# Attention: five of twenty key tiles' probabilities summed on VectorE instead of three, and two more steps ahead of the second maxima's transposes

## The chip, the cores and the metric

The kernel runs on one core of one Trainium2 chip. The metric is the device time of one execution in microseconds. Engines are called PE (TensorE), DVE (VectorE), ACT (ScalarE), POOL (GpSimd) and SP (SyncE, which only issues DMAs here). SBUF is the on-chip memory, PSUM the accumulator memory that PE writes.

## The reference

One layer of a diffusion backbone: a combined projection, attention beside a state space, an output projection and an FFN. 2048 latent and 256 context tokens; attention has 8 query heads, 2 key/value heads and head size 64. All in float32. The change concerns the attention alone, in which a latent query sees 2048 latent keys and 512 cached context keys (20 tiles of 128 keys), a context query the 256 context keys (2 tiles):

```python
def one_block(q_blk):
    s = jnp.einsum("bqkgd,bskd->bkgqs", q_blk, k, preferred_element_type=jnp.float32) * scale
    p = jax.nn.softmax(s, axis=-1).astype(v.dtype)
    return jnp.einsum("bkgqs,bskd->bqkgd", p, v)
```

## The kernel before

The program runs in stages: projections (to about 460 us), attention with the state space's scans beside it (to about 1505 us), the state space's GLU, the output projection, and a long FFN. This section is about the attention stage.

**Units.** Attention is cut into 20 units (`units`, L176): a unit is a pair of heads and a block of 512 latent or 256 context queries. 16 are latent (20 key tiles each), 4 are context units (2 tiles). They are numbered ui = 0 to 19; the context units are 0, 2, 4 and 6, and the last is 19.

**What a unit does.** For each key tile j, `scores` (L260) multiplies keys by queries into PSUM tile st (L267, L268; two matmuls per head, since the operands are split into a rounded part and its remainder), and ACT writes the exponentials into an SBUF tile p of 128 keys x 2 heads x 512 queries (L270). There are 11 buffers of p. `values` (L275) multiplies p with the values into pv (L284; the keys are contracted by PE). The softmax's denominator needs the sum over all p tiles of a unit. It is made by adding the tiles element by element: one running sum on DVE (L294, one 128x1024 add per tile) and one on POOL (L297, two 128x512 adds per tile). The first tile that goes to an engine isn't added; its buffer becomes the running sum. `VJ` (L305) lists the tiles of a latent unit that go to DVE; the last unit has a rule of its own. `finish` (L308) adds the two sums (L313, DVE) and contracts them with ones (L318, PE), takes the reciprocal through a DMA round trip, and scales pv (L336).

**What must be there before a unit starts.** The exponentials need each query's maximum over all keys. `prep` (L179) makes it for the unit ahead: it splits the queries (L219, L222), multiplies them with the keys a second time (L197, PE) and reduces each 128x512 block to a column of maxima (L198, DVE); `pmx` has three PSUM buffers for these blocks. `close` (L201) reduces a head's columns (L204, DVE) and writes the negated maximum into zb (L205, ACT); `put` (L207) transposes zb on PE (L210), and ACT copies it into the lower rows of ql (L211), where it joins the scores' second matmul.

**The order.** In this stage PE and DVE run in the order in which the program is written (`manual_schedule`, L1148); ACT, POOL and SP are ordered by a scheduler. `attend` (L347) writes it: groups of four tiles; first the scores of the next group, then the values of this one, so that the adds of tiles 8 to 11 are written after the scores of tiles 12 to 15. `prep` is a generator, and a `yield` in it is a step; after each score tile (a slot) `attend` lets it go st["per"] steps further, so that the steps of the units ahead are spread over this unit's 20 slots. `prep_steps` (L341) gives their number. The state space (`ssm_gen`, L944) and the GLU's first loads (`glu_front`, L1088) are generators too, one step per slot and one after each group's values.

Of the kernel before, what the change touches and what calls it, by code (L numbers as in the profile page):

```python
# [48 lines left out]
def build(nc, tc, I, O):  # L49
# [129 lines left out]
    def prep(ui, late=0):  # L179
        kv, tok, nq, k0, k1, pr_ = units[ui]  # L180
        khl, kho = KK[kv, k0]
        ntq = nq // 128
        nkc = (k1 - k0 + 3) // 4
        qs = X["kc"].tile([128, 4, 2, 2, 64], F32, name="qs", bufs=1)
        for h in range(2):
            src = q_scr[tok:tok + nq, 4 * kv + 2 * pr_ + h].rearrange("(i p) d -> p i d", p=128)
            for d in range(2):
                X["dma"].dma_start(out=qs[:, 0:ntq, h, d, :], in_=src)
        res, mxs = [], []

        def maxes(h, cs):
            qh, khl = res[h][0], KK[kv, k0][0]
            for i in range(ntq):
                for c in cs:
                    a, b = 512 * c, min(512 * c + 512, (k1 - k0) * 128)
                    sp_ = X["pmx"].tile([128, 512], F32, name="m")
                    PE.matmul(sp_[:, 0:b - a], qh[:, i * 128:(i + 1) * 128], khl[:, a:b], start=True, stop=True)  # L197
                    V.tensor_reduce(mxs[h][:, i, c:c + 1], sp_[:, 0:b - a], axis=AX.X, op=ALU.max)  # L198
                    yield

        def close(h):  # L201
            z = X["zb"][h % 2]
            m4 = X["kc"].tile([128, 4], F32, name="m4", bufs=2)
            V.tensor_reduce(m4[:, 0:ntq], mxs[h][:, 0:ntq, 0:nkc], axis=AX.X, op=ALU.max)  # L204
            S.activation(z[:, 0:ntq, 64], m4[:, 0:ntq], AF.Copy, scale=-1.0)  # L205

        def put(h):  # L207
            tp = X["pmx"].tile([128, 512], F32, name="m")
            for i in range(ntq):
                PE.transpose(tp[:, i * 128:(i + 1) * 128], X["zb"][h % 2][:, i, :], ident)  # L210
            S.copy(res[h][1][64:128, 0:nq], tp[64:128, 0:nq])  # L211

        yield
        for h in range(2):
            qh, ql = (X["kc"].tile([128, nq], F32R, name=f"{n}{h}_{nq}", bufs=2 if nq > 256 else 1) for n in ("qh", "ql"))
            tp = X["pmx"].tile([128, 512], F32, name="m")
            for i in range(ntq):
                PE.transpose(tp[:, i * 128:(i + 1) * 128], qs[:, i, h].rearrange("p a b -> p (a b)"), ident)
            S.copy(qh[:, 0:nq], tp[:, 0:nq])  # L219
            if ui > 1:  # L220
                yield
            V.tensor_sub(ql[0:64, 0:nq], tp[0:64, 0:nq], qh[0:64, 0:nq].bitcast(F32))  # L222
            res.append((qh, ql))
            mxs.append(X["kc"].tile([128, 4, 6], F32, name="mx", bufs=2))
            yield
        if ui > 1:
            yield from maxes(0, range(nkc))
            close(0)
            second = maxes(1, range(nkc))
            for _ in range(min(6, 2 * nkc)):  # L230
                next(second)
                yield
            put(0)
            yield
            yield from second
            close(1)
            yield
            yield
            yield
            put(1)  # L240
            yield
            QT[ui] = res
            return
        for h in range(2):
            yield from maxes(h, range(nkc - late))
            if not late:
                close(h)
        if late:
            yield "rest"
            for h in range(2):  # L250
                yield from maxes(h, range(nkc - late, nkc))
                close(h)
        for h in range(2):
            put(h)
            yield
        QT[ui] = res
# [18 lines left out]
    def values(ui, j):  # L275
# [14 lines left out]
        else:  # L290
            e = "v" if j in VJ else "g"
        if e in acc:
# [9 lines left out]
            S.copy(pvs[:, 0:nq], pv[:, 0:nq])  # L302
            PEND.append((ui, pvs, acc))

    VJ = (4, 11, 19)  # L305
    PEND = []

    def finish():  # L308
# [31 lines left out]

    def prep_steps(ui):  # L341
        kv, tok, nq, k0, k1, pr_ = units[ui]
        n = 2 * (nq // 128) * ((k1 - k0 + 3) // 4) + 10
        first = next(i for i, u_ in enumerate(units) if (u_[0], u_[3]) == (kv, k0))
        return n + (1 + (k1 - k0 + 3) // 4 if ui == first else 0)

    def attend(B, Sg):  # L347
# [10 lines left out]
        def slot(ui, j):  # L358
            while st["ready"] < ui:
                step()  # L360
            lat = units[ui][2] > 256
            if lat and not j:
                st["goal"] = min(ui + (2 if ui + 1 < 2 * len(cu) else 1), len(units) - 1)
                st["per"] = sum(prep_steps(i) for i in range(st["ready"] + 1, st["goal"] + 1)) / 19.5
                st["q"] = 0.0
            scores(ui, j)
            st["q"] += st["per"] if lat else 0.0
            while st["q"] >= 1.0:
                st["q"] -= 1.0
                if st["ready"] < st["goal"]:  # L370
                    step()
            if lat:
                X["pos"] = "p"
                next(Sg, None)
# [22 lines left out]
    with ExitStack() as pa:  # L397
# [489 lines left out]

        def bg():
            g = dict(c=kbuild(0, 20, 22), k=kbuild(0, 0, 20, (0, 4, 8, 12)), p=prep(0))
            X["dma"] = nc.scalar  # L890
            for ch in "cpk":
# [4 lines left out]
            for ch in "cpkp":  # L896
                next(g[ch])
                yield
            p = prep(1, 1)
            next(p)  # L900
            for ch in "ppkppkk":
# [14 lines left out]
            for ui in range(2, len(units)):  # L916
                kv, k0, k1 = units[ui][0], units[ui][3], units[ui][4]
                if (kv, k0) not in KK:
                    yield from kbuild(kv, k0, k1)
                yield from prep(ui)  # L920
                yield ui
# [797 lines left out]
```

## Time and profile before

| what | value |
|---|---|
| median of 3 runs | 3349.92 us (3345.46 to 3354.12) |
| profiled execution, its own time | 3348.23 us |
| its span, first to last instruction | 3346.3 us |
| mean granted TensorE clock | 0.965 |
| PE busy | 3066.9 us, 92% of the span |
| DVE busy | 2530.4 us, 76% |
| POOL busy | 1933.8 us, 58% |
| ACT busy | 1343.0 us, 40% |

The shares are means over stages with different limits. A row of the profile names an engine, a line of the kernel, the tiles written and read (out<-in) and their sizes; "idle before" is the time for which the engine stood still ahead of the instruction, with what ended it. A granted clock of 1.00 is 2.4 GHz, 0.50 is 1.2 GHz.

### The profile page before, as it was taken

What the parts mean: (1) busy time and instruction counts of PE and PEld (TensorE: products, weight loads), DVE (VectorE), ACT (ScalarE), POOL (GpSimd) and SP (SyncE); (2) the same over time, 40 slices, a digit from 0 to 9 for tenths busy, and PEclk for the clock granted to TensorE, in tenths of its full rate; (3) what the DMA queues carried; (4) which work ended last, traced back from release to release, by engine and by line L of the source; (5) the groups of instructions that cost most, each with busy time, mean ns of one, the idle gap of its engine ahead of it and who ended that gap; (6) DMA issues with size and microseconds to landing.
All of it is one profiled execution on the core that took longest, in us unless ns stands there. A gap on an engine that the chain in (4) does not pass through costs nothing. (4 is left out here: it accounts for less than half of the span.)

```text
span 3346.3 us, 46314 instructions
## 1 busy us (share of the span) xinstructions
PE 3066.9 (92%) x16087; PEld 2479.5 (74%) x16087; DVE 2530.4 (76%) x3414; ACT 1343.0 (40%) x2378; POOL 1933.8 (58%) x1433
## 2 busy tenths in 40 slices
PE   7898888999999999886997999999999999999897
PEld 5787664565655665545776999999999998878686
DVE  4889766767777777667777877887788877567887
ACT  4333333444444444534555433433343434232332
POOL 3777535666785787664434544554455556354675
PEclk9999999999999999998998999999999999999899
DMA  7565442323333322204565444444434445658653
GB/s 264 188 198 186 144 121 49 87 76 86 84 81 87 84 72 50 64 20 145 176 188 190 140 117 120 132 132 121 119 101 125 127 129 169 164 147 201 175 205 138
DMA packets 515380, 435.20 MB, mean 130 GB/s; under 512 B 106374, under 2 KB 449454, under 8 KB 515148
## 3 DMA queue, kind: packets, MB, share of 16 engines
q1 hardware_dynamic: 498060, 400.57, 39.8%
q0 software_dynamic: 5184, 18.88, 3.3%
q10 hardware_dynamic: 11904, 12.82, 1.1%
q8 instruction: 127, 2.08, 0.3%
q14 instruction: 105, 0.86, 0.1%
HBM read 279.37 MB, written 143.73 MB: 126 GB/s over the span
## 5 line engine op out<-in xcount | busy, mean ns | idle before, releaser
L297 POOL TENSOR_TENSOR p<-p 128x512 f32<-128x512 f32 x502 | 699.0, 1431 | 281.5 <-PE pv L284 177.1
L89 POOL TENSOR_TENSOR op<-wr,op 128x512 fp32r<-128x512 f32 (+1 forms) x297 | 413.3, 1398 | 427.9 <-ACT op L88 386.6
L94 PE MATMUL o<-h,op 128*128 128x384 f32 x1848 | 624.0, 338 | 17.1 <-ACT h L88 16.4
L95 PE MATMUL o<-h,op 128*128 128x384 f32 x1848 | 624.2, 338 | 16.4 <-DVE h L89 16.4
L96 PE MATMUL o<-h,op 128*128 128x384 f32 x1848 | 622.8, 337 | 0.0
L198 DVE TENSOR_REDUCE mx<-m 128x1 f32<-128x512 f32 (+1 forms) x656 | 405.2, 674 | 145.4 <-PE m L197 143.7
L270 ACT ACTIVATE p<-st 128x1024 f32<-128x1024 f32 (+1 forms) x328 | 330.3, 1015 | 285.6 <-PE st L268 278.4
L88 ACT CAST op<-sw 128x512 fp32r<-128x512 f32 (+1 forms) x381 | 232.9, 613 | 331.8 <-PE o L95 267.8
L95 PEld LDWEIGHTS o<-h,op 128*128 128x128 f32 x1848 | 351.4, 190 | 18.8 <-DVE h L89 18.6
L94 PEld LDWEIGHTS o<-h,op 128*128 128x128 f32 x1848 | 351.0, 190 | 18.8 <-ACT h L88 17.9
L96 PEld LDWEIGHTS o<-h,op 128*128 128x128 f32 x1848 | 351.2, 190 | 0.0
L89 POOL TENSOR_TENSOR op<-sw,op 128x512 fp32r<-128x512 f32 (+1 forms) x177 | 259.4, 1469 | 121.8 <-ACT op L88 121.8
L88 ACT CAST op<-wr 128x512 fp32r<-128x512 f32 (+1 forms) x333 | 199.0, 608 | 255.9 <-PE o L95 170.4
L284 PE MATMUL pv<-p,vall 128*64 128x512 f32 (+1 forms) x1312 | 296.4, 594 | 0.0
L95 PE MATMUL o<-fvm,op 128*128 128x512 f32 x693 | 278.6, 402 | 18.6 <-DVE fvm L89 9.4
L94 PE MATMUL o<-fvm,op 128*128 128x512 f32 x693 | 277.1, 401 | 10.0 <-ACT fvm L88 8.0
L197 PE MATMUL m<-khl,qh 128*128 128x512 f32 (+1 forms) x656 | 232.8, 425 | 56.4 <-DVE mx L198 47.4
L267 PE MATMUL st<-qh,khl 128*128 128x512 f32 (+1 forms) x656 | 276.4, 422 | 6.7 <-ACT p L270 6.0
L96 PE MATMUL o<-fvm,op 128*128 128x512 f32 x693 | 275.1, 398 | 0.0
L268 PE MATMUL st<-ql,kho 128*128 128x512 f32 (+1 forms) x656 | 259.2, 396 | 0.0
L197 PEld LDWEIGHTS m<-khl,qh 128*128 128x128 f32 x656 | 125.4, 191 | 131.0 <-DVE mx L198 99.8
L284 PEld LDWEIGHTS pv<-p,vall 128*64 128x64 f32 x1312 | 86.9, 137 | 156.8 <-issue 153.6
(314 smaller groups left out, 6287.2 us busy)
## 6 DMA issues: line engine op xcount, KB each, us to landing
wr<-w_ffn_in SPq DMA_DIRECT2D x132, 512.0 KB
wm<-w_mod SPq DMA_DIRECT2D x48, 512.0 KB
act_scr<-s SPq DMA_DIRECT2D x99, 192.0 KB
wr<-act_scr SPq DMA_DIRECT2D x36, 512.0 KB
x_scr<-gy POOLq DMA_DIRECT2D x36, 512.0 KB, 6.4
xt<-x SPq DMA_DIRECT2D x34, 512.0 KB
act_scr<-gy SPq DMA_DIRECT2D x90, 192.0 KB
sw<-act_scr SPq DMA_DIRECT2D x54, 256.0 KB
```

Of the source, the lines that this page charges most:

```text
L88: a = (copy or S.copy)(hi, src)
L89: b = (sub or V).tensor_sub(lo, src, hi.bitcast(F32))
L94: PE.matmul(out, ah, bh, start=first, stop=False)
L95: PE.matmul(out, ah, bl, start=False, stop=False)
L96: return PE.matmul(out, al, bh, start=False, stop=last)
L197: PE.matmul(sp_[:, 0:b - a], qh[:, i * 128:(i + 1) * 128], khl[:, a:b], start=True, stop=True)
L198: V.tensor_reduce(mxs[h][:, i, c:c + 1], sp_[:, 0:b - a], axis=AX.X, op=ALU.max)
L267: PE.matmul(st[:, h, 0:nq], khl[:, kc], qh[:, 0:nq], start=True, stop=False)
L268: PE.matmul(st[:, h, 0:nq], kho[:, kc], ql[:, 0:nq], start=False, stop=True)
L270: S.activation(p[:, :, 0:nq], st[:, :, 0:nq], AF.Exp, scale=0.125)
L284: PE.matmul(pv[64 * h:64 * h + 64, 0:nq], X["vall"][:, k0 + j, 64 * kv:64 * kv + 64], p[:, h, 0:nq], start=j == 0, stop=j == nk - 1)
L297: G.tensor_add(acc[e][:, h, 0:nq], acc[e][:, h, 0:nq], p[:, h, 0:nq])
```

## The change

Two edits. `VJ` gets five tiles instead of three: 3, 7, 11, 15 and 19, the last of each group of four. So the DVE sum starts with tile 3 and has four adds in a unit instead of two; POOL has 14 tiles to add instead of 16, 28 instructions instead of 32. This holds for 15 latent units; the last latent unit and the context units keep their rules. And in `prep` five steps instead of three lie between the second head's `close` and its `put`, with `prep_steps` raised by two.

```diff
@@ prep
             yield from second
             close(1)
-            yield
-            yield
-            yield
+            for _ in range(5):
+                yield
             put(1)
@@ attention
-    VJ = (4, 11, 19)
+    VJ = (3, 7, 11, 15, 19)
@@ prep_steps
-        n = 2 * (nq // 128) * ((k1 - k0 + 3) // 4) + 10
+        n = 2 * (nq // 128) * ((k1 - k0 + 3) // 4) + 12
```

The new file is one line shorter, so that lines behind `prep` have a number lower by one there: L270 is L269, L294 is L293, L313 is L312, L330 is L329, L336 is L335.

DVE in unit 18, from the final sum of unit 17 on, before (mx<-m are the block maxima, m<-mx a head's `close`, p<-p an add of tiles):

```order
L313 TENSOR_TENSOR p<-p 128x1024
L198 TENSOR_REDUCE mx<-m 128x1 x5
L204 TENSOR_REDUCE m_12814<-mx 128x4
L198 TENSOR_REDUCE mx<-m 128x1 x15
L294 TENSOR_TENSOR p<-p 128x1024
L330 RECIPROCAL rr<-rr 128x8
L198 TENSOR_REDUCE mx<-m 128x1 x5
L204 TENSOR_REDUCE m_12986<-mx 128x4
L336 TENSOR_TENSOR pvs<-pvs,rT 128x512
```

The same place now:

```order
L312 TENSOR_TENSOR p<-p 128x1024
L198 TENSOR_REDUCE mx<-m 128x1 x4
L204 TENSOR_REDUCE m_12777<-mx 128x4
L198 TENSOR_REDUCE mx<-m 128x1 x6
L293 TENSOR_TENSOR p<-p 128x1024
L198 TENSOR_REDUCE mx<-m 128x1 x10
L293 TENSOR_TENSOR p<-p 128x1024
L329 RECIPROCAL rr<-rr 128x8
L198 TENSOR_REDUCE mx<-m 128x1 x4
L204 TENSOR_REDUCE m_12950<-mx 128x4
L293 TENSOR_TENSOR p<-p 128x1024
L335 TENSOR_TENSOR pvs<-pvs,rT 128x512
```

Between the final sum and the add of tile 11 stood 20 maxima; now an add (of tile 7) parts them into 10 and 10, and another (of tile 15) stands behind the second `close`.

ACT at the end of unit 9, where the maxima of unit 10 are closed, before (p<-st are the exponentials, zb the negated maxima, ql the copy after `put`):

```order
L270 ACTIVATE p<-st 128x1024 x3
L1007 COPY s<-h_5217 128x4
L1008 ACTIVATE s<-h_5217 128x4
L270 ACTIVATE p<-st 128x1024 x4
L205 ACTIVATE zb_4606<-m_8435 128x4
L211 CAST ql_512_8008<-m 64x512
L270 ACTIVATE p<-st 128x1024
```

The same place now:

```order
L269 ACTIVATE p<-st 128x1024 x3
L1006 COPY s<-h_5217 128x4
L1007 ACTIVATE s<-h_5217 128x4
L269 ACTIVATE p<-st 128x1024 x3
L205 ACTIVATE zb_4606<-m_8417 128x4
L269 ACTIVATE p<-st 128x1024
L211 CAST ql_512_7998<-m 64x512
L269 ACTIVATE p<-st 128x1024
```

zb stood behind the fourth exponential, the unit's last; now it stands ahead of it.

## Rows read from the trace of the kernel before

**Rows 1.** Stretch, us, busy us of PE, PEld, DVE, ACT, POOL; clock, DMA share, GB/s

```profile
460.00:1505.00 1045.00, 958.04 (x4450) 578.85 (x4451) 729.42 (x926) 462.54 (x721) 721.08 (x519) 0.98 0.28 74
```

**Rows 2.** Waits of PE, 460 to 1505 us: total us, times, longest us

```profile
PE m L197 <- DVE mx L198: 43.8, 21, 13.1
PE m L210 <- ACT zb L205: 18.8, 15, 2.7
PE st L267 <- ACT p L270: 6.0, 9, 1.4
```

**Rows 3.** Groups by line, 460 to 1505 us: busy us, mean ns, idle before

```profile
L297 POOL TENSOR_TENSOR p<-p 128x512 f32<-128x512 f32 x502 | 699.0, 1431 | 281.5 <-PE pv L284 177.1 <-ACT p L270 104.5
...
L294 DVE TENSOR_TENSOR p<-p 128x1024 f32<-128x1024 f32 x37 | 82.8, 2239 | 14.4 <-PE pv L284 12.0 <-ACT p L270 2.2
```

**Rows 4.** Timeline of PE: start us, us, instruction, idle before it

```profile
526.09 2.59 PE L197 MATMUL m<-khl,qh 128*128 128x512 f32 x4 [9.66 <-DVE mx L198]
...
1360.88 0.80 PE L197 MATMUL m<-khl,qh 128*128 128x512 f32 x1 [8.59 <-DVE mx L198]
...
1439.76 1.39 PE L197 MATMUL m<-khl,qh 128*128 128x512 f32 x2 [13.09 <-DVE mx L198]
```

**Rows 5.** Timeline of DVE

```profile
511.51 11.65 DVE L294 TENSOR_TENSOR p<-p 128x1024 f32<-128x1024 f32 x1
...
578.75 5.76 DVE L1033 TENSOR_TENSOR s<-s,et 128x584 f32<-128x584 f32 x1
...
1353.97 6.25 DVE L89 TENSOR_TENSOR wgl<-raw,wgh 128x512 fp32r<-128x512 f32 x1 [8.31 <-ACT wgh L88]
...
1400.00 2.30 DVE L313 TENSOR_TENSOR p<-p 128x1024 f32<-128x1024 f32 x1
...
1421.50 17.54 DVE L294 TENSOR_TENSOR p<-p 128x1024 f32<-128x1024 f32 x1
```

**Rows 6.** Timeline of POOL (instructions without a pause between them in one row)

```profile
484.97 37.11 POOL L297 TENSOR_TENSOR p<-p 128x512 f32<-128x512 f32 x30 [11.95 <-PE pv L284]
...
561.02 22.86 POOL L297 TENSOR_TENSOR p<-p 128x512 f32<-128x512 f32 x18 [23.29 <-PE pv L284]
...
1331.04 28.64 POOL L297 TENSOR_TENSOR p<-p 128x512 f32<-128x512 f32 x22 [15.50 <-ACT p L270]
...
1399.94 38.01 POOL L297 TENSOR_TENSOR p<-p 128x512 f32<-128x512 f32 x30 [16.77 <-ACT p L270]
```

**Rows 7.** Timeline of POOL and DVE around 1297 us

```profile
1269.28 46.25 POOL L297 TENSOR_TENSOR p<-p 128x512 f32<-128x512 f32 x32 [6.24 <-PE pv L284]
...
1281.29 1.85 DVE L1053 TENSOR_TENSOR r<-r,rw 128x584 f32<-128x584 f32 x1
...
1297.49 1.46 DVE L294 TENSOR_TENSOR p<-p 128x1024 f32<-128x1024 f32 x1
```

**Rows 8.** Timeline of DVE: maxima behind an idle time, where new adds come to stand

```profile
1226.78 1.36 DVE L198 TENSOR_REDUCE mx<-m 128x1 f32<-128x512 f32 x2 [1.14 <-PE m L197]
...
1285.98 1.36 DVE L198 TENSOR_REDUCE mx<-m 128x1 f32<-128x512 f32 x2 [2.84 <-PE m L197]
...
1414.67 1.36 DVE L198 TENSOR_REDUCE mx<-m 128x1 f32<-128x512 f32 x2 [4.62 <-PE m L197]
```

**Rows 9.** Busy time by stretch, columns as in the first group

```profile
526.10:532.00 5.90, 5.90 (x13) 4.10 (x14) 4.67 (x8) 1.02 (x1) 0.33 (x1) 0.50 0.13 22
...
1439.80:1443.40 3.60, 3.60 (x8) 2.71 (x9) 2.47 (x5) 0.42 (x1) 0.00 (x0) 0.50 0.24 63
```

**Rows 10.** Timeline at the end of unit 9

```profile
867.13 1.95 ACT L270 ACTIVATE p<-st 128x1024 f32<-128x1024 f32 x2 [0.54 <-PE st L268]
...
867.55 0.39 PE L268 MATMUL st<-ql,kho 128*128 128x512 f32 x1
868.98 0.20 ACT L205 ACTIVATE zb<-m 128x4 f32<-128x4 f32 x1
...
869.23 0.66 PE L210 MATMUL m<-ident,zb 128*128 128x128 f32 x4 [1.29 <-ACT zb L205]
```

## Prediction, made before the change was run

> **What bounds the kernel now.** I read the stage first, then the waits inside it, then the rows behind the longest waits. The change touches only the attention stage, from 460 to 1505 us. In that stage TensorE (PE) is busy 958.0 of 1045 us, GpSimd (POOL) 721.1, VectorE (DVE) 729.4 and ScalarE 462.5 [rows 1]. So PE sets the time, and what an edit can win is at most the 87 us in which PE stands still, plus what a lower clock costs behind such gaps. PE's waits say who makes them [rows 2]: 43.8 us for DVE's row maxima (L198), 18.8 us for the zb copy of ScalarE (L205), 6.0 us for the exponentials (L270). None of them names POOL. POOL's 502 half-tile adds at 1431 ns [rows 3] are off PE's path, and taking work from POOL is worth something only through DVE.
>
> That path exists. Three rows hold 31.3 of the 43.8 us: PE waits 9.66, 8.59 and 13.09 us for one maximum each [rows 4]. Each time DVE was inside one single instruction that should take about a microsecond: 11.65 us and 17.54 us for a 128x1024 add (L294), 6.25 us for a 128x512 subtraction (L89); a fourth, L1033 at 578.75, took 5.76 us, and no PE gap follows it [rows 5]. In each case DVE comes free about when a long unbroken row of POOL adds ends: 484.97 + 37.11 = 522.08 against 523.16, 561.02 + 22.86 = 583.88 against 584.51, 1331.04 + 28.64 = 1359.68 against 1360.22, 1399.94 + 38.01 = 1437.95 against 1439.04 [rows 5, 6]. So a DVE instruction with two SBUF operands can be passed over by POOL until POOL has nothing left to do. Mostly it is not: the add at 1297.49 took 1.46 us in the middle of POOL's 46.25 us row [rows 7]. What differs is how long POOL had run undisturbed. At 1297.49 the last two-operand instruction of DVE had ended at 1283.14, 14.4 us earlier, and DVE got its turn. Passed over were those that came 26.5 us after POOL's start (511.51), 17.7 us after it (578.75) and, at 1421.50, 19.2 us after the L313 that ended at 1402.30 [rows 5, 6, 7]. I looked at every such meeting in the stage: none up to 14.4 us is passed over, and beyond 17 us there are only these four. I take that as the rule of this kernel; why the chip does so no row shows.
>
> The Trainium skill states it otherwise (page "SBUF — State Buffer", section "Who interferes with whom"): a DVE instruction with two SBUF inputs contends with a GpSimd instruction that reads SBUF, and the shared ports are an exclusive lock held for one whole instruction, so that the loser waits for that one. By that rule DVE would wait for one POOL add at most, and no number of DVE adds would cure a long wait; the 17.54 us, in which some 13 POOL adds went by, do not agree with it [rows 5]. What the time would be if regular DVE adds cured nothing is the first rival.
>
> **The change part by part.**
>
> *Adds moved from POOL to DVE.* 15 units change (all latent ones but the last). Each loses two tiles on POOL, four half adds: 60 x 1.43 us = 86 us of POOL's time [rows 3], which by itself is worth nothing, since nobody on PE's path waits for it except through the 11 p buffers, which ScalarE's exponentials need free. PE waits 6.0 us for the exponentials [rows 2]. I take half as won, 3 us; the ends are 0 and 6.0.
>
> Each unit gets two more adds on DVE, after tiles 7 and 15 (tile 3 only starts the sum in place of tile 4): 30 adds of 1.2 us free or 2.3 us when a POOL add is in front. Their cover is the burst of 16 value matmuls and the scores behind it, in which DVE waits for PE: after L1053 at 1281.29 it idles 2.84 us [rows 7, 8], which holds 2.3. The tightest place I found is 1226.78, where instructions of the state space leave 1.14 us [rows 8]; there an add costs 2.3 - 1.1 = 1.2 us. At the other new place, the end of a unit, DVE idles longer, since it waits for ScalarE's copy of the next queries. Some three units of 15 are tight: 3 us lost. If the cover were gone everywhere it would be 30 x 1.2 = 36 us, the upper end; the lower is 0.
>
> *What they do to the long waits.* The adds now come after every group of four tiles (7, 11, 15, 19), and the final sum L313 after the next unit's first group, so that DVE meets POOL about every 12 us: below 14.4. I expect the long waits behind PE's three gaps to go.
> - Unit 18, 1421.50: the add of tile 7 lands near 1411, where DVE idled 4.62 us anyway [rows 8]; the add of tile 11 then gets its turn in about 2 us. PE's 13.09 us go whole. So does the half clock behind them: at 1439.80 to 1443.40 PE was busy throughout at a granted clock of 0.50 (1.2 instead of 2.4 GHz), having stood idle before; 3.6 us of work done in 3.6 that take 1.8 [rows 9]. Together 15 us.
> - Unit 1, 511.51: with an add of tile 7 near 497 the add at 511.51 takes 2.3 instead of 11.65 us. Behind it stand L330 and three state-space instructions, which ran beside an idle POOL and would now take some 1.85 us each, as at 1281.29 beside POOL [rows 7]: the maxima resume at 511.5 + 2.3 + 0.2 + 5.55 = 519.6. PE's maximum then comes at about 520 and not at 526.09. 6 us, and of the 2.95 us that the half clock cost (5.90 us at 0.50 [rows 9]) I take 1: 7 us.
> - Unit 17, 1353.97: L89 waited 8.31 us for ScalarE first [rows 5], and still will. Then 2.3 instead of 6.25 us: 4 us, and 1 for the clock: 5 us.
>
> That is 27 us; the ends are 0 (the first rival) and 31.3 + 2.95 + 1.8 = 36 us (the gaps and both half clocks gone).
>
> *Two more steps.* Fifteen times PE waits for zb, 18.8 us in all [rows 2], mostly 1.29 us as at 869.23. There the order tells why: zb stands on ScalarE behind the last two exponentials, 867.13 to 869.08, and PE's transposes come right after the scores of the last of them [rows 10]. The two extra steps, spread over the same 20 slots (52 / 19.5 = 2.67 steps a slot instead of 50 / 19.5 = 2.56), put the last maximum two steps earlier, and on ScalarE zb now goes ahead of the unit's last exponential; I count eight units in which that happens, and some had it already. zb then ends about 0.2 us after the last but one exponential, near 868.3, and PE, done with its scores at 867.94, waits 0.4 instead of 1.29: 0.9 us x 8 = 7, with 1 more for the unit whose wait was 2.7: 8 us. Ends: 0 and 18.8. Nothing is queued behind: the later copy of the put (L211) has a burst of value matmuls before the next scores need it.
>
> **The sum.** -3 + 3 - 27 - 8 = -35 us against the profiled execution's own 3348.2 us: 3313 us. The median of the runs shown is 1.7 us above that execution, less than the rest is uncertain. What follows the stage is tied to its end (the last unit's normalisation frees the memory that the output projection's weights need), so I let the gain through whole.
>
> **The rivals.**
> 1. *The long waits are not cured*, only moved: which of the two engines gets the ports is a matter of phase, or POOL's rows of adds are not the cause. For it: only four cases, and a page that knows no such passing over. Against: no exception among all meetings in the stage. The time: 3348 - 8 - 3 + 3 = 3340.
> 2. *Slower: more adds, more passing over.* If each L294 runs the same risk whatever came before, 2 of 37 were passed over [rows 3, 5], so 30 more bring 1.6 further, each at the cost of the two seen, (9.66 + 13.09) / 2 = 11.4 us and some 2.4 of half clock: 13.8 us. 1.6 x 13.8 = +22, with rival 1's -8: 3362. It decides from the first new add of tile 7 or 15 that lasts over 5 us while PE needs a maximum. Against: the new adds come 12 us after the one before.
> 3. *DVE's queue is the bound*: the adds cost 1.2 us each since the cover is used up. +33 more than taken: 3346. For it: DVE is busy 70% of the stage and PE waits already behind such pile-ups; against: the idle times of [rows 8].
> 4. *The extra steps move nothing on PE's path* (PE waits for the last exponential instead of zb): then 8 us less won, 3321; within the forecast's own range.
>
> **How the numbers follow.** The forecast with its spread (3290 to 3328) gets 0.71, rival 1 0.15, rival 2 0.07, rival 3 0.07. Rival 2 and half of rival 3 may lie outside the range, and some of the far side; 3288 to 3343 leaves out under 2 in 10. A measurement of this kernel can tell about 0.3%, 10 us, from no change, so faster means under 3338: the forecast's 0.71 and half of rival 1 make 0.78. The other half and rival 3 make 0.15 for the same, rival 2 0.07 for slower.
>
> **What would show it.** In the profile after: L297 down to 442 adds and L294 up by 30; no DVE add over about 3 us in units 1, 17 and 18; PE's wait for L198 down from 43.8 to about 20 us, that for zb from 18.8 to about 10. If long DVE instructions remain in the middle of POOL's rows with less than 14.4 us since DVE's last, the rule is wrong and rival 1 or 2 holds. If there are none and PE's wait for L198 has not fallen, rival 3 holds. If the stage shrinks by 35 us and the whole does not, what follows was tied to something else.

## The result and the profile after

The change took 3313.37 us (median of 4 runs, 3312.63 to 3319.35) where the kernel before took 3351.26 beside it (4 runs, 3345.46 to 3354.12): a ratio of 0.9898, 95% interval 0.987 to 0.9926. It is faster, by about 35 us (38 by the medians, 34 by the ratio). The profiled execution's span is 3310.9 us (before 3346.3), its mean granted clock 0.972 (before 0.965).

The first view is the attention stage in one row (us; busy time of PE, PEld, DVE, ACT, POOL; clock; DMA share; GB/s). It answers to [rows 1]: the stage ends near 1480 instead of 1505 us. POOL's busy time fell from 721 to 672 us while DVE's rose from 729 to 751, and PE's stayed at about 960.

```profile
460.00:1480.00 1020.00, 964.00 (x4479) 582.44 (x4480) 750.64 (x961) 464.29 (x725) 671.63 (x459) 0.99 0.29 76
```

The second is PE's waits in that stretch (us in total, times, longest), to be read against [rows 2]: the wait for the maxima fell from 43.8 to 16.5 us and its longest from 13.1 to 3.2, that for zb from 18.8 to 7.2. The wait for the exponentials rose from 6.0 to 8.8.

```profile
PE m L197 <- DVE mx L198: 16.5, 29, 3.2
PE st L266 <- ACT p L269: 8.8, 11, 3.2
PE m L210 <- ACT zb L205: 7.2, 11, 1.3
PE m L1012 <- DVE mx L198: 6.8, 14, 2.3
```

The third is the groups by line (busy us, mean ns), against [rows 3]: 442 adds on POOL instead of 502, and 67 on DVE instead of 37, whose mean fell from 2239 to 1706 ns although there are more of them.

```profile
L296 POOL TENSOR_TENSOR p<-p 128x512 f32<-128x512 f32 x442 | 647.0, 1502 | 286.7 <-PE pv L283 185.7 <-ACT p L269 101.0
...
L293 DVE TENSOR_TENSOR p<-p 128x1024 f32<-128x1024 f32 x67 | 114.3, 1706 | 7.6 <-PE pv L283 5.2 <-ACT p L269 2.2
```

The fourth is DVE's timeline (start, duration, both us) at the places of the long instructions of [rows 5], in units 1, 3, 17 and 18. In this execution none lasts over 3 us: 1.21 instead of 11.65, 2.71 where L1033 took 5.76 at 578.75, 1.47 instead of 6.25, and 1.24 (the add of tile 11 at 1408.04) instead of 17.54. The new adds of tile 7 in units 1 and 18 are those at 498.38 and 1396.56.

```profile
498.38 1.22 DVE L293 TENSOR_TENSOR p<-p 128x1024 f32<-128x1024 f32 x1
...
514.45 1.21 DVE L293 TENSOR_TENSOR p<-p 128x1024 f32<-128x1024 f32 x1
...
568.82 2.71 DVE L293 TENSOR_TENSOR p<-p 128x1024 f32<-128x1024 f32 x1
...
1346.15 1.47 DVE L89 TENSOR_TENSOR wgl<-raw,wgh 128x512 fp32r<-128x512 f32 x1 [6.37 <-ACT wgh L88]
...
1396.56 1.79 DVE L293 TENSOR_TENSOR p<-p 128x1024 f32<-128x1024 f32 x1
...
1408.04 1.24 DVE L293 TENSOR_TENSOR p<-p 128x1024 f32<-128x1024 f32 x1
...
1414.42 2.06 DVE L293 TENSOR_TENSOR p<-p 128x1024 f32<-128x1024 f32 x1
```

POOL's rows beside two of them show that the cure has two halves. In unit 1 the new add at 498.38 breaks POOL's row, and with fewer adds the row ends at 486.08 + 28.25 = 514.33, just ahead of the add at 514.45, which so meets nobody. In unit 3 the add at 568.82 still waits for the row's end, 550.02 + 20.43 = 570.45, as the prediction's rule has it after 18 us without a turn; only the end is near.

```profile
486.08 28.25 POOL L296 TENSOR_TENSOR p<-p 128x512 f32<-128x512 f32 x22 [12.78 <-PE pv L283]
...
550.02 20.43 POOL L296 TENSOR_TENSOR p<-p 128x512 f32<-128x512 f32 x16 [19.01 <-PE pv L283]
```

**Where the time came from.** The table splits each profiled execution. The stage runs from the first score matmul to the last scaling of pv. "Idle" is the sum of PE's gaps in it; "half clock" is half of PE's busy time in the stretches granted 0.50, the time that they cost; "mx" is the part of the idle time that stood ahead of L197, whoever ended it. "Rest" is what follows the stage, up to the end of the span.

| run | stage | idle | mx | zb | half clock | rest |
|---|---|---|---|---|---|---|
| before | 1049.8 | 87.6 | 52.7 | 18.8 | 11.8 | 1838.9 |
| the change | 1020.6 | 56.4 | 26.8 | 7.3 | 11.5 | 1832.4 |
| e1_adds | 1019.9 | 63.0 | 29.5 | 17.0 | 6.8 | 1838.3 |
| e2_steps | 1067.7 | 97.9 | 70.9 | 7.3 | 20.1 | 1843.1 |
| e3_unspaced | 1075.4 | 97.8 | 66.6 | 8.7 | 30.0 | 1836.3 |
| e4_touch | 1046.8 | 79.6 | 49.5 | 7.8 | 16.3 | 1837.9 |
| e5_touch_often | 1067.2 | 92.0 | 57.8 | 18.8 | 20.2 | 1836.3 |
| e7_nine | 1029.0 | 56.1 | 34.7 | 3.1 | 11.6 | 1837.7 |
| e8_change_again | 1016.0 | 54.5 | 25.8 | 7.4 | 8.0 | 1838.8 |
| e10_whole | 1076.9 | 101.1 | 58.4 | 15.9 | 28.4 | 1842.3 |
| e11_change_whole | 1081.3 | 98.0 | 60.8 | 6.2 | 32.9 | 1837.3 |
| e12_touch_wide | 1036.7 | 71.3 | 37.5 | 8.0 | 12.4 | 1840.7 |

A row is one execution, and the experiments ran on four chips, on which the kernel before isn't equally fast. So a difference between rows isn't the edit's alone: e10's span is 30 us longer than that of the kernel before, but its ratio, taken on one chip, says 8 us. e1's row is the fastest of its five runs (3318.43 us, median 3325.99), e2's lies 11 us above its median.

The stage gave 29.2 us and the rest 6.4. Matching PE's instructions one by one, the change is 11 us ahead behind unit 1's gap, loses 5 again between 600 and 750 us, wins 6 at unit 17 and 16 at unit 18.

The 5 us that are lost show what a new add costs where little covers it. DVE's timeline of the change: the new add of a tile 7 took 2.31 us beside POOL at 711.26, and from there on DVE had no idle time up to the add of tile 11 at 723.12, behind which a scaling and a state-space product queue.

```profile
711.26 2.31 DVE L293 TENSOR_TENSOR p<-p 128x1024 f32<-128x1024 f32 x1
...
723.12 2.29 DVE L293 TENSOR_TENSOR p<-p 128x1024 f32<-128x1024 f32 x1
...
727.12 1.73 DVE L1052 TENSOR_TENSOR r<-r,rw 128x584 f32<-128x584 f32 x1
```

The same three queue in the kernel before, at 730.88 and as long, but there DVE had idled 1.65 and 0.47 us ahead of them, and PE's wait behind them was 0.51 us. Its DVE timeline:

```profile
724.07 1.36 DVE L198 TENSOR_REDUCE mx<-m 128x1 f32<-128x512 f32 x2 [1.65 <-PE m L197]
...
730.88 2.33 DVE L294 TENSOR_TENSOR p<-p 128x1024 f32<-128x1024 f32 x1
```

PE's timeline in the change: it stood still for 2.27 us, waiting for a maximum.

```profile
729.50 1.56 PE L1012 MATMUL m<-ut,mst 128*128 128x144 f32 x8 [2.27 <-DVE mx L198]
```

Behind this gap, and behind one of 3.21 us at 1058, PE worked at 0.50 (1.2 GHz). The stretches (columns as in the first view):

```profile
730.30:733.70 3.40, 3.40 (x12) 2.91 (x11) 0.81 (x2) 1.82 (x4) 3.40 (x4) 0.50 0.19 41
1061.40:1064.80 3.40, 3.40 (x8) 2.72 (x9) 2.27 (x4) 2.81 (x4) 0.00 (x0) 0.50 0.89 204
```

So the long half-clock stretches behind units 1, 17 and 18 are gone ([rows 9] are two of them), but new short ones took their place: the stage lost 11.5 us to them instead of 11.8.

### The profile page after: what moved, and what is told of

The parts are those of the page before. It is cut to its first block, busy times and chain, and to the rows that moved or that the text cites. A ratio compares the mean times of both kernels' runs of the same rounds, so it can differ in the third digit from the quotient of the medians.

```text
span 3310.9 us, 46264 instructions
## 1 busy us (share of the span) xinstructions
PE 3059.0 (92%) x16087; PEld 2468.7 (75%) x16087; DVE 2547.8 (77%) x3444; ACT 1341.8 (41%) x2378; POOL 1888.8 (57%) x1373
## 5 line engine op out<-in xcount | busy, mean ns | idle before, releaser
L296 POOL TENSOR_TENSOR p<-p 128x512 f32<-128x512 f32 x442 | 647.0, 1502 | 286.7 <-PE pv L283 185.7
L269 ACT ACTIVATE p<-st 128x1024 f32<-128x1024 f32 (+1 forms) x328 | 331.4, 1016 | 245.5 <-PE st L267 236.3
L197 PE MATMUL m<-khl,qh 128*128 128x512 f32 (+1 forms) x656 | 230.0, 422 | 30.5 <-DVE mx L198 20.2
L197 PEld LDWEIGHTS m<-khl,qh 128*128 128x128 f32 x656 | 124.3, 191 | 103.5 <-DVE mx L198 67.7
```

The source lines that it names most:

```text
L269: S.activation(p[:, :, 0:nq], st[:, :, 0:nq], AF.Exp, scale=0.125)
L296: G.tensor_add(acc[e][:, h, 0:nq], acc[e][:, h, 0:nq], p[:, h, 0:nq])
```

## The experiments

Theory: what counts is how long POOL runs without a two-operand DVE instruction between; the change is faster since its adds come at every fourth tile. Rivals: it is the smaller load on POOL, or the two steps. Line numbers in experiments with five steps are those of the change, as far as the first line that an experiment adds. Each ratio is to the kernel before on the same chip, where its medians were 3356 us (e1 to e4), 3359 (e5, e7, e8), 3371 (e10, e11) and 3358 (e12).

**e1_adds: the five tiles alone, three steps as before.**

```diff
-    VJ = (4, 11, 19)
+    VJ = (3, 7, 11, 15, 19)
```

> The five tiles on DVE alone, three steps as before. Theory (spacing: a two-operand DVE instruction is passed over only after some 15 us of undisturbed POOL adds): the long waits in units 1, 17 and 18 go, PE's wait for L198 falls from 43.8 to about 20 us, PE's wait for zb stays near 18.8 us; 3320 to 3328 us, about 25 us under the kernel before. Rival (the two steps made most of the gain): less than 12 us under it, 3338 or more.

3325.99 us, ratio 0.991 (0.989 to 0.9931). PE's waits (same columns as above):

```profile
PE m L197 <- DVE mx L198: 17.7, 20, 3.5
PE m L210 <- ACT zb L205: 17.0, 15, 1.3
```

The maxima's wait falls as in the change, zb's stays. The tiles alone bring most of the gain (0.991 against the change's 0.9898, and 0.9879 in its second measurement, e8).

**e2_steps: the two steps alone.**

```diff
-            yield
-            yield
-            yield
+            for _ in range(5):
+                yield
...
-        n = 2 * (nq // 128) * ((k1 - k0 + 3) // 4) + 10
+        n = 2 * (nq // 128) * ((k1 - k0 + 3) // 4) + 12
```

> The two steps alone, tiles 4, 11 and 19 on DVE as before. Theory: the long DVE instructions stay (one of over 10 us in unit 18 at least), PE's wait for L198 stays at 35 us or more, its wait for zb falls to some 8 us; 3338 to 3346 us. Rival (the steps made most of the gain): 3325 us or less.

3364.71 us, ratio 1.0023 (1.0003 to 1.0044): slower by little, a miss. PE's wait for zb does fall, but that for the maxima rises from 43.8 to 62.1:

```profile
PE m L197 <- DVE mx L198: 62.1, 34, 13.0
...
PE m L210 <- ACT zb L205: 7.1, 11, 1.3
```

DVE's timeline tells why: another instruction, which before got its turn, is now passed over (14.67 us), beside the one of unit 18. It came only 11.8 us and 9 POOL adds behind the last DVE instruction with two SBUF operands (L1052), less than the 14.4 us up to which the prediction's rule has none passed over.

```profile
1109.03 14.67 DVE L1032 TENSOR_TENSOR s<-s,et 128x584 f32<-128x584 f32 x1
...
1444.62 17.39 DVE L293 TENSOR_TENSOR p<-p 128x1024 f32<-128x1024 f32 x1
```

What the steps win at zb, they lose by shifting who meets POOL when.

**e3_unspaced: the change's load and steps, with the five tiles not spaced.**

```diff
-    VJ = (3, 7, 11, 15, 19)
+    VJ = (4, 9, 11, 18, 19)
```

> Five tiles on DVE and five steps as in the change, so four DVE adds and 28 POOL adds in a unit, but as tiles 4, 9, 11, 18 and 19: the adds come two at a time, some 24 us apart, as far apart as before. Theory (spacing): passing over comes back, one DVE instruction of over 8 us in unit 18 and one in unit 1 or 17, PE's wait for L198 35 us or more; 3338 to 3350 us. Rival (load: fewer adds on POOL, or more on DVE, whatever their places): no DVE add over 4 us in these units, 3312 to 3322 us.

3374.14 us, ratio 1.0066 (1.0041 to 1.0091). POOL has 14 tiles and DVE four adds in a unit, as in the change, and the kernel is slower than before. One add of unit 18 alone (duration in ns):

```profile
L293 DVE TENSOR_TENSOR p<-p x1: 14958/14958/14958, 1453.6 to 1453.6; 128x1024 f32<-128x1024 f32 x1
```

So the load by itself doesn't remove unit 18's long wait; where the adds stand does. It isn't the whole of e3's time, though: the long ones of units 1 and 17 are gone, three adds of 4.50 to 5.77 us came at other places, and two adds that come together also make DVE's queue longer, which was not tried apart.

**e4_touch and e5_touch_often: small DVE adds instead of real ones.** Can an add of 128x8 of tiles of its own, nearly free, break POOL's rows? In e4, on top of e2, after tiles 7 and 15 of the 15 units:

```diff
+        if nk > 4 and ui + 1 < len(units) and j in (7, 15):
+            V.tensor_add(X["tc"][0], X["tc"][1], X["tc"][2])
```

> Tiles 4, 11 and 19 on DVE and 32 POOL adds in a unit as before, five steps as in the change, and a two-operand DVE add of 128x8 on tiles of its own where the change adds tiles 7 and 15. Nothing of its result is used. Theory (spacing): the short adds keep POOL's undisturbed stretches below 15 us, the long DVE instructions in units 1, 17 and 18 go with POOL's load unchanged, PE's wait for L198 about 20 us or less; 3310 to 3322 us. Rival (load): the long ones stay, 3338 us or more.

3353.56 us, ratio 0.9998 (0.9979 to 1.0017): a miss. Unit 18's long add is gone, others stay, such as this one on DVE's timeline:

```profile
1055.41 8.21 DVE L293 TENSOR_TENSOR p<-p 128x1024 f32<-128x1024 f32 x1
```

In e5 the kernel before got such an add after every second tile:

```diff
+            if lat and j % 2 and ui + 1 < len(units):
+                V.tensor_add(X["tc"][0], X["tc"][1], X["tc"][2])
```

> The kernel before (tiles 4, 11, 19; three steps; 32 POOL adds in a unit) with a two-operand DVE add of 128x8 on tiles of its own after every second score tile of the 15 units; nothing of its result is used. The touches come some 6 us apart. Theory (spacing, as a likelihood that grows with POOL's undisturbed time: in the runs so far 2 of some 480 meetings up to 13 us were passed over by two adds or more, 9 of 19 from 13 to 16 us, 11 of 14 beyond): no DVE instruction over 4 us is left in the units, PE's wait for L198 is below 28 us, 3318 to 3332 us. Rival (POOL's load): long ones stay, 3345 us or more.

3367.07 us, ratio 1.0014 (0.9996 to 1.0031), the theory's second miss. On DVE's timeline of unit 18 two of the small adds got their turn and the third waited 14.29 us:

```profile
1418.90 2.26 DVE L313 TENSOR_TENSOR p<-p 128x1024 f32<-128x1024 f32 x1
...
1424.45 0.38 DVE L368 TENSOR_TENSOR tc<-tc,tc 128x8 f32<-128x8 f32 x1
...
1427.95 0.62 DVE L368 TENSOR_TENSOR tc<-tc,tc 128x8 f32<-128x8 f32 x1
...
1435.12 14.29 DVE L368 TENSOR_TENSOR tc<-tc,tc 128x8 f32<-128x8 f32 x1
...
515.35 1.32 DVE L294 TENSOR_TENSOR p<-p 128x1024 f32<-128x1024 f32 x1
```

It waited from 14 us behind L313's end to the end of POOL's row, 1418.81 + 30.58 = 1449.39. "Any meeting breaks the row" is wrong; here the small adds did not count. In unit 1 it went otherwise: the add of tile 11 took 1.32 us (the last line above) where 11.65 us stood [rows 5], 22 POOL adds into the row and with no two-operand instruction of DVE's between but small adds. Why they sufficed there, no run tells.

**e6_meet: the meeting by itself.** POOL runs a row of 30 adds of 128x512, or 60 of 128x256; DVE reduces PSUM blocks, n of 128x512 and s short ones, and then makes a 128x1024 add, the probe.

```python
for i in range(30 * 512 // w):
    G.tensor_add(acc[:, i % 2, 0:w], acc[:, i % 2, 0:w], p[:, i % 2, 0:w])
...
V.tensor_add(a, a, q)
```

> A measurement by itself; nothing of the layer is computed and the outputs are zeros. POOL makes rows of 30 adds of 128x512 (or 60 of 128x256) in place without a wait; DVE reduces PSUM for 2 to 28 us meanwhile and then makes one two-operand add of 128x1024. Theory (undisturbed time decides): with 128x512 adds the DVE add takes up to 2.6 us if it comes within 12 us of the row's start, and lasts to the row's end in most cases beyond 16 us; with 128x256 adds the turn comes at the same time if time decides, at half of it if the number of POOL adds decides. Rival (phase alone): passed over as often early as late, or never.

Two probes of the 128x512 rows and two of the 128x256 rows on DVE's timeline, each pair the last that was granted and the first that was not:

```profile
978.32 2.08 DVE L77 TENSOR_TENSOR a<-a,q 128x1024 f32<-128x1024 f32 x1
...
1016.78 21.31 DVE L77 TENSOR_TENSOR a<-a,q 128x1024 f32<-128x1024 f32 x1
...
2002.18 1.72 DVE L77 TENSOR_TENSOR a<-a,q 128x1024 f32<-128x1024 f32 x1
...
2046.15 31.47 DVE L77 TENSOR_TENSOR a<-a,q 128x1024 f32<-128x1024 f32 x1
```

POOL's rows began at 962.22, 1000.41, 1993.25 and 2035.70. In the 128x512 rows every probe up to +16.10 us took 1.23 to 2.39 us, and all 16 from +16.37 us on lasted to the row's end; at the last granted and at the first passed over 14 adds had begun. In the 128x256 rows the edge lies between +8.92 (14 begun) and +10.45 us (16 begun), and all 18 probes behind it were passed over. So here it is the number of POOL's instructions that decides, not the time, and not the columns added either (14 instructions of 256 or of 512). The Trainium skill (page "SBUF — State Buffer", section "Who interferes with whom") has the loser wait for one whole instruction; up to 14 adds the 1.23 to 2.39 us agree with it, beyond them 31.47 us don't.

**e7_nine and e8_change_again.** e7 is the change with nine steps instead of five (`prep_steps` +16), e8 the change once more beside it.

> The change with nine steps instead of five ahead of the second put. If PE's wait for zb is worth its time, it falls from 7.3 to below 3 us and the time by 4 us or more against the change run beside it. If steps only move PE's waits elsewhere (theory by now: the two steps of the change took 10 us of zb and gave them back), the time is the same within 5 us or longer.

> The change itself again, for a comparison on one chip. Theory (the adds made all of it): its ratio to the kernel before is that of the adds alone, 0.991, within 0.003. Rival (the two steps add their 10 us): 0.987 or lower.

e7: 3325.22 us, ratio 0.9893 (0.987 to 0.9915); e8: 3319.34, ratio 0.9879 (0.9852 to 0.9905). Nine steps take zb's wait to 3.1 us and give the time back ahead of the maxima's matmuls (34.7 against 25.8 us idle there), though not by waits for the maxima themselves, which fell from 15.2 to 10.8 us: PE's wait for the next queries' ql rose from 1.6 to 9.7 us and that for rT from 1.5 to 5.8. With e1 at 0.991 and its interval overlapping e8's, the steps' own share of the change is up to some 10 us or nothing; these runs don't tell which.

Both profiles show an add that is passed over for longer than any in the change's own profile. In e8, which is the change, the add of tile 11 in the fifth latent unit waited to the end of POOL's row, 12.7 us and 10 POOL adds behind the last two-operand instruction; no PE gap follows it. In e7 an add at 642.44 took 7.15 us, 12 adds into a row. DVE's timeline of e8:

```profile
790.96 4.32 DVE L293 TENSOR_TENSOR p<-p 128x1024 f32<-128x1024 f32 x1
```

In the change's profile six two-operand instructions met POOL behind 10 or more of its adds, and only the one at 568.82 was passed over. So the change lies close to the edge, and is not clear of it.

**e9_reset: which small add starts the count anew?** As e6, with a row of 34 adds, and an add of 128 x w on the way to the probe.

```python
if w:
    V.tensor_add(af[:, 0:w], af[:, 0:w], qf[:, 0:w])
```

> A measurement by itself, as e6_meet: nothing of the layer is computed and the outputs are zeros. GpSimd runs a row of 34 adds of 128x512 (about 42.5 us) without pause; VectorE reduces PSUM blocks, adds once a piece of 128 x w of its own SBUF tiles (w = none, 8, 64, 128, 256, 512, 1024), reduces on, and then makes the probe, an add of 128x1024. Four placings, two trials of each width: 12 reductions ahead of the small add and 18 behind, 18 and 12, 6 and 24, and 9 and 30; 56 trials. Without a small add the probe comes about 17.5 us into the row (in the last placing about 22 us), where e6_meet has it waiting for the row's end. Theory (the count of GpSimd's instructions starts anew only behind a VectorE instruction that really held GpSimd up, as in e5_touch_often, where adds of 128x8 changed nothing): in the first three placings probes behind w = 512 and 1024 last 1.2 to 2.4 us, those behind none and w = 8 last to the row's end, 15 us or more, and the switch lies somewhere between 64 and 256. Rival A (any meeting starts the count anew, and e5_touch_often has another cause): every probe behind a small add, w = 8 too, lasts 1.2 to 2.4 us in the first three placings. Rival B (nothing starts it anew while GpSimd runs on): all last to the row's end. In the fourth placing, where more than 14 adds lie between the small add and the probe, every probe lasts to the row's end by all three.

DVE's timeline of two trials of the first placing, w = 8 and w = 64; in both the small add met POOL and the probe came 8 adds later:

```profile
143.42 0.51 DVE L78 TENSOR_TENSOR a<-a,q 128x8 f32<-128x8 f32 x1
154.62 24.53 DVE L81 TENSOR_TENSOR a<-a,q 128x1024 f32<-128x1024 f32 x1
...
186.52 0.57 DVE L78 TENSOR_TENSOR a<-a,q 128x64 f32<-128x64 f32 x1
197.78 1.29 DVE L81 TENSOR_TENSOR a<-a,q 128x1024 f32<-128x1024 f32 x1
```

In the first three placings all 12 probes behind w = 0 or 8 lasted to the row's end (24.46 to 24.98 us), and all 30 behind w = 64 or more took 1.21 to 1.36 us. The switch lies lower than expected, between 8 and 64 columns, and "it must hold POOL up" is wrong in that form, as POOL's rows show. They are those of w = 8, 64 and 1024 in the first placing:

```profile
136.55 41.52 POOL L74 TENSOR_TENSOR acc<-acc,p 128x512 f32<-128x512 f32 x34
...
179.65 42.50 POOL L74 TENSOR_TENSOR acc<-acc,p 128x512 f32<-128x512 f32 x34
...
526.00 43.48 POOL L74 TENSOR_TENSOR acc<-acc,p 128x512 f32<-128x512 f32 x34
```

The row of w = 1024 holds two DVE adds of 128x1024 that got their turn, the small one and the probe, and is 1.96 us longer than an undisturbed one: 0.98 for each. The row of w = 64 is longer by the probe's 0.98 alone, so its small add held POOL up by nothing measurable. The last placing, expected to be passed over throughout, was split: w = 0, 8 and 64 were (18.52 to 19.46 us), w = 128 and more took 1.42. There 14 adds had begun since the small one's end, the very edge of e6, so whether 64 columns counted there can't be told. Why 8 columns don't count, no row shows.

**e10_whole and e11_change_whole: half as many instructions for the same work.** POOL adds a tile in one 128x1024 instruction; e10 is otherwise the kernel before, e11 the change.

```diff
-                for h in range(2):
-                    G.tensor_add(acc[e][:, h, 0:nq], acc[e][:, h, 0:nq], p[:, h, 0:nq])
+                G.tensor_add(acc[e][:, :, 0:nq], acc[e][:, :, 0:nq], p[:, :, 0:nq])
```

> The kernel before, with GpSimd adding each tile in one instruction of 128x1024 instead of two of 128x512: about 251 adds of about 2.5 to 2.9 us in the stage; the same work, half as many instructions, VJ and steps as before. Theory (what e6_meet showed: the number of GpSimd's instructions decides, some 14 to 16, and not the time): the rows of 30 halves become rows of 15, so that hardly any row is long enough; the long VectorE instructions of units 1, 17 and 18 go (none over 6 us, where a wait for one whole add alone gives up to 4), PE's wait for the maxima falls from about 44 to 20 to 30 us, the stage from 1050 to 1020 to 1035 us, the ratio to before 0.99 to 0.995. Rival (time or work without a turn decides, about 13 to 16 us): the long ones stay, at 10 to 20 us, the stage stays at 1045 to 1060 and the ratio is 1.00 or above, since each meeting now also waits up to 2.5 us instead of 1.25.

> The change, with GpSimd adding each tile in one instruction of 128x1024 instead of two of 128x512: 14 adds in a unit instead of 28. Both theories expect no long VectorE instruction here (none over 5 us), as in the change. What it tells is the price of a longer hold: each two-operand VectorE instruction that meets GpSimd waits for up to 2.5 us instead of 1.25. If VectorE's cover is as wide as the prediction took it, the ratio to before is that of the change, 0.985 to 0.992; if VectorE's queue is the tighter one (the prediction's third rival), PE's wait for the maxima rises by 10 us or more above the change's 26.8 and the ratio is 0.993 or above.

e10: 3381.35 us, ratio 1.0023 (1.0009 to 1.0037), a miss in time; e11: 3380.57, 1.002 (1.0004 to 1.0036), as its second case has it. Of the mechanism e10 shows what was asked, on DVE's timeline in units 1 and 18:

```profile
511.15 1.51 DVE L294 TENSOR_TENSOR p<-p 128x1024 f32<-128x1024 f32 x1
...
1460.07 2.45 DVE L294 TENSOR_TENSOR p<-p 128x1024 f32<-128x1024 f32 x1
```

These come 26.5 us into POOL's row and 18.1 us behind L312, as late as the two that took 11.65 and 17.54 us before [rows 5], and both got their turn behind 11 and 7 adds. So in the kernel too it isn't the time. (Whole adds also leave POOL some 0.1 us between two, halves none; that this gap lets DVE in is not excluded here.) The time went the other way, since each meeting now waits for an add of 2.57 us in the mean instead of 1.43. The groups of e10 (busy us, mean ns); the final sum L312 took 1746 ns in the kernel before:

```profile
L296 POOL TENSOR_TENSOR p<-p 128x1024 f32<-128x1024 f32 x251 | 645.1, 2570 | 331.8 <-PE pv L284 196.1 <-ACT p L270 119.0
...
L312 DVE TENSOR_TENSOR p<-p 128x1024 f32<-128x1024 f32 x16 | 36.8, 2300 | 0.1
```

In e11 no DVE instruction with two SBUF operands lasted over 3.6 us, and yet PE's wait for the maxima was 42.0 us against the change's 16.5:

```profile
PE m L197 <- DVE mx L198: 42.0, 34, 3.7
```

DVE's cover, the time in which it waits for PE anyway, is thin: 34 waits of PE of up to 3.7 us cost about as much as the few long ones of before (43.8), and the half clock cost 32.9 us of the stage instead of 11.5, though not in runs side by side.

**e12_touch_wide: e4 with small adds of 128x112.**

```diff
-            V.tensor_add(X["tc"][0], X["tc"][1], X["tc"][2])
+            V.tensor_add(X["tc"][0], X["tc"][0], X["tc"][1])
...
-    X["tc"] = [wk.tile([128, 8], F32, name=f"tc{i}") for i in range(3)]
+    X["tc"] = [wk.tile([128, 112], F32, name=f"tc{i}") for i in range(2)]
```

> The kernel of e4_touch (VJ=(4,11,19) as before, five steps, a small VectorE add of own tiles after tiles 7 and 15 of 15 latent units), with the small add 112 columns wide instead of 8; nothing else differs. GpSimd keeps its 16 tiles. Theory (e9_reset: an add of 64 columns or more starts the count of GpSimd's instructions anew, one of 8 does not): the long VectorE instructions that e4_touch still had (8.21, 7.0, 6.5, 4.97, 4.1 us) go, none over 4 us except where no small add came within 14 GpSimd adds; PE's wait for the maxima falls from 49.5 to 25 to 33 us, the stage from 1046.8 to 1018 to 1030 us, and the ratio to before is 0.988 to 0.993, that of the change, though no work has left GpSimd. Rival (it is GpSimd's smaller load that cured the change, or the real adds' length of a whole add): long ones of 5 us and more remain as in e4_touch and the ratio stays at 0.997 to 1.003.

3341.55 us, ratio 0.995 (0.9934 to 0.9966): between what the theory and the rival expected, and faster than e4's 0.9998. The 30 adds cost the same as those of 8 columns (856 ns in the mean against 882), all five long ones of e4 are gone, and one other came; PE's wait for the maxima falls from 40.5 to 28.0 us and that for the exponentials rises from 6.9 to 11.7. DVE's timeline and PE's waits:

```profile
1294.25 8.30 DVE L293 TENSOR_TENSOR p<-p 128x1024 f32<-128x1024 f32 x1
```

```profile
PE m L197 <- DVE mx L198: 28.0, 31, 6.7
PE st L266 <- ACT p L269: 11.7, 11, 3.9
```

The one of 8.30 us came 13.7 us and 11 POOL adds behind the last DVE instruction of two operands. Two others with the same 13.7 us were granted. It did not last to the row's end either: POOL ran on without a pause for 6.4 us behind it. So the kernel's edge is softer than e6's: over all runs instructions were passed over from 9 adds (e2) on and granted up to 14 (e3, at 577.21). POOL's load seems to matter a second time, since two tiles less make its rows shorter; that this is what e12 lacks is argued and was not tried apart. Breaking the rows without taking load from POOL is worth about half of the change's gain, with one long wait and the price of the small adds left in it.

## Why the prediction was right, point by point

- **The sum.** -35 us forecast, -35 in the profiled executions (3346.3 to 3310.9). That they agree so closely is in part luck. The stage gave 29 and what follows it 6, which no term of the sum had, and in the stage a larger gain at the long waits covers losses at the adds and the p buffers. Why 6 us came behind the stage is open: the half clock there cost 28.1 us instead of 39.5, but in e1 it cost 26.7 and its rest is that of before (1838.3). e8's stage was 34 us shorter and its rest the same as before (1838.8 against 1838.9), so the 6 us behind the stage need not be the change's doing.
- **The long waits, -27.** The step that carries the result, and it holds: all three gaps gone, -11, -6 and -16 where -7, -5 and -15 stood. Unit 1 gave more since POOL's shorter row had ended by then, so that L1032 to L1034 took 0.7 to 0.8 us each and not 1.85. The rule behind it was right in what to do (the change against e3: same load and steps, 0.9898 against 1.0066) and wrong in its quantity: in place of 14.4 to 17 us of POOL's time stand, by e6, 14 to 15 POOL instructions. Its safe bound was too wide: at 11.8 us in e2 and at 12.7 us in e8 (the change once more) instructions were passed over, and less than 14.4 us is what the prediction names as the sign that the rule is wrong. So a spacing of 12 us makes long waits rarer, and that the one in e8 met no PE gap may be luck. (The instruction at 578.75 came 17.0 us, not 17.7, behind DVE's last one, L1053.)
- **The 30 adds, +3.** Too low. What is left of PE's waits for maxima without the three long gaps rose from 43.8 - 31.3 = 12.5 to 16.5 us at L197, and the wait ahead of the state space's L1012 from 3.9 to 6.8: +7, as at 729.50 us. e11 shows how steep this term is once each meeting costs 2.5 us.
- **The p buffers, -3.** This step failed: PE's wait for the exponentials went up by 2.8 us, and ACT, which should have waited less for POOL to free a p buffer, waited longer. ACT's wait before and in the change:

```profile
ACT p L270 <- POOL p L297: 4.8, 9, 0.6
...
ACT p L269 <- POOL p L296: 6.0, 6, 1.5
```

  The longest wait for the exponentials, 3.21 us at 1058, has another cause: a small copy of the state space, ahead of the exponentials on ACT, writes a tile that a scan on DVE still read, and began at 1059.95, 0.08 us behind the scan's end (the profile names no releaser). The scan stood behind a scaling (L335) for which DVE had idled 6.13 us until the reciprocals' DMA landed. Why fewer POOL adds did not free buffers sooner was not tried.
- **The two steps, -8.** zb's wait fell by 11.6 us, more than forecast, in the way that [rows 10] gave. How much of it reached the time is open: by the ratios of e1 (0.991), the change (0.9898) and e8 (0.9879) it is 4 to 10 us, with intervals that overlap; by the stages (1019.9 without the steps, 1020.6 and 1016.0 with them) it is -1 to 4, but e1's is that of its fastest run. So neither the forecast's 8 nor the fourth rival (3321) is excluded. Alone the steps cost time (e2), which no rival had: they change which DVE instruction comes late into a POOL row.
- **The rivals.** The first fell with the three gaps. The second, more adds and more passing over, did not show in the change's time: one add of 4.32 us in e8, with no PE gap behind it. With the same number of adds in other places, e3, long ones came. The third, DVE's queue, is real in small here and in full in e11.

## What to carry to other kernels

Where VectorE and GpSimd both add SBUF tiles, look for single VectorE instructions that last many times their group's shortest and end with GpSimd's row; less load alone did not remove them (e3); they came behind an unbroken row, here of some 9 to 15 instructions or more. Place VectorE's own two-operand work at even distances inside such rows before moving more of it, and count each meeting as a wait for the GpSimd instruction under way, so keep those short. An edit that only shifts the order is to be tried together with what it shifts: two steps alone cost 0.2% here; with spaced adds they gained 0.1 to 0.3% by the ratios, which is not clear of nothing.

## What the runs showed of the hardware that was not expected

- In the measurement by itself (e6) a VectorE add of two SBUF operands got its turn after the GpSimd add under way (1.23 to 2.39 us) as long as 13 GpSimd adds or fewer had begun without a turn, and in two of three cases at 14; from then on it waited until GpSimd stopped, 31.47 us at most, and its phase against the adds played no part. In the layer's kernels the edge lay anywhere from 9 to 14 adds, and some of those passed over got their turn inside the row (8.30 us in e12).
- In e9 a VectorE add of 128x64 started the count anew and one of 128x8 did not (1.29 against 24.53 us for the probe), though neither made GpSimd's row measurably longer. In e5 adds of 128x8 failed in unit 18 and did not in unit 1.
- Gaps of 2.27 and 3.21 us were followed by 3.4 us at the granted clock 0.50 with PE busy throughout. In e10 and e11, where no VectorE instruction of two SBUF operands lasted over 3.6 us, the half clock cost 28.4 and 32.9 us of the stage, against 11.8 in the profile of the kernel before, which did not run beside them.
